# Places in SBUF: two pools trade places, odd-sized tiles are put together, V weight rows become 640 columns wide

## The chip, the cores and the metric

The kernel runs on one core of one Trainium2 chip. The metric is the device time of one execution in microseconds (us), lower is better. The kernel before took 1538.11 us as the median of three runs (1535.11, 1538.11 and 1538.29); the execution that the profiler recorded took 1535.44 us.

## The reference

One decoder layer over 1024 tokens of width 1024, all in float32. Two attentions run side by side and are merged by gates; a SwiGLU feed-forward network follows. Cut to what matters:

```python
h = rms_norm(x, norm_mix_g[layer])
proj = h @ w_in[layer]                      # q, k, v of both attentions, forget logits, gates
...
o_g, lse_g = dilated_window_attention(...)  # three groups (window, dilation), four heads each
y_a = o_a.reshape(b, s, DIL_OUT_WIDTH).astype(x.dtype) @ w_dil_out[layer]
o_b = forgetting_attention(fox[:, :, 0], fox[:, :, 1], fox[:, :, 2], jax.nn.log_sigmoid(f_logit))
y_b = o_b.reshape(b, s, FOX_WIDTH).astype(x.dtype) @ w_fox_out[layer]
x = x + (g_a * y_a + g_b * y_b).astype(x.dtype) @ w_out[layer]
h2 = rms_norm(x, norm_ffn_g[layer])
gu = h2 @ w_ffn_in[layer]                   # 1024 -> 2 x 2816
x = x + (jax.nn.silu(gu[..., :D_FF]) * gu[..., D_FF:]) @ w_ffn_down[layer]
return rms_norm(x, norm_final_g)
```

The forgetting attention adds a running sum of `log_f` over the tokens to its scores; the kernel computes that sum with a triangular matrix of ones (`upper`).

## The kernel before, in words

**Products in three parts.** A float32 operand is split into a rounded high part and the rest, both of type fp32r (`split`, lines 91 to 93: ScalarE writes the high part, VectorE the low one). A product is then three matmuls: high by high, high by low, low by high (`mm3`, `projT`, `prod`). Nearly all of TensorE's work is such matmuls of 128 x 128 weights with a moving operand of 512 columns. Each is a load of its weights (PEld in the profile) and a matmul (PE); the load for the next matmul runs while the matmul before it streams its columns.

**Stages, in order of time.** (1) Tokens are normalised and transposed into `hT_t`, which stays in SBUF as moving operand; V of the forgetting attention is computed beside it (`values`), there with `hT_t` as weights and the V weights `wv` as moving operand of 256 and 264 columns. (2) The running sum of the forget logits. (3) Forgetting attention, four pairs of heads; q and k come from `projT` with weights from `wpool`. (4) Dilated attention. (5) Gates and merge (`merge`, weights from `wpool`). (6) The output projection (`w_out`), here with `hT_t` as weights and `w_out` as moving operand, of `w_out` the first four of eight tiles in the contraction out of `wpool`. (7) The feed-forward products: two plain columns of tiles (`plain`), then twenty in a scheme of seven products (`up`), of which the two with `A1` take their weights from `wpool`. (8) The down projection, added up in nine groups; the first group uses `wpool` for both operands.

**Filler.** `ahead` computes q and k of the dilated attention and the gates in advance: 28 calls, each 2 halves of the weights by 2 halves of the tokens by 4 tiles by 3 matmuls, from its own pool at the right end of SBUF (`fw`), into its own two banks (`pf`). They are scheduled between the work of stages 1 to 5.

**Order.** A scheduler at build time sets each engine's order; at run time an engine takes its instructions in that order and waits on semaphores.

**Places.** Pools are stacked: those on the left side from low addresses up, in the order in which they are entered (lines 72 to 76: `cpool`, `wpool`, `small`, `hpool`), those on the right side from the end down. A tile takes a multiple of 32 bytes of each partition. Below, *residue* is a tile's byte address in a partition modulo 512. `cpool` holds `ident` (512 bytes), `epst` (32), `ones` (512), `bg` (64) and `bf` (32), 1152 together, so what comes behind it has another residue than what stands before it. In the right-hand pools no tile has an odd size, but SBUF's end has residue 480. `load_w` (line 103) allocates a weight tile of `kt` rows of `n` columns; for V of the forgetting attention `n` is 520, so a row is 2080 bytes, and each next row's residue is 32 more.

Of the kernel before, what the change touches and what calls it, by code (L numbers as in the profile page):

```python
# [8 lines left out]
F32 = mybir.dt.float32  # L9
F32R = mybir.dt.float32r  # L10
I32 = mybir.dt.int32
AF = mybir.ActivationFunctionType
ALU = mybir.AluOpType
PSUM = bass.MemoryType.PSUM

P = 128
# [3 lines left out]
NT = S // P  # L20
# [27 lines left out]
def layer_kernel(  # L48
# [16 lines left out]
    nc = tc.nc  # L65
    x, out, w_in, w_dil_out, w_fox_out = x[0], out[0], w_in[0], w_dil_out[0], w_fox_out[0]
    w_out, w_ffn_in, w_ffn_down = w_out[0], w_ffn_in[0], w_ffn_down[0]

    def pool_of(name, bufs, side="left"):
        return tc.tile_pool(name=name, bufs=bufs, side=side, reuse_waits="tile")  # L70

    cpool = ctx.enter_context(tc.tile_pool(name="cpool", bufs=1))
    wpool = ctx.enter_context(tc.tile_pool(name="wpool", bufs=2))
    small = ctx.enter_context(tc.tile_pool(name="small", bufs=4))
    h_ctx = pool_of("hpool", 1)
    hpool = h_ctx.__enter__()
    psd = ctx.enter_context(tc.tile_pool(name="psd", bufs=6, space=PSUM))
# [6 lines left out]
    def nm(s):  # L84
        uid[0] += 1
        return f"{s}_{uid[0]}"

    def pd():
        return psd.tile([P, HALF], F32, tag="d", name=nm("pd"))
# [13 lines left out]
    def load_w(src, kt, n, tag="w", bufs=2, pool=None, chunk=None, rpool=None, rbufs=2, shared=0, between=None):  # L103

        pool = pool or wpool
        hi = pool.tile([P, kt, n], F32R, tag=tag + "h", name=nm("wh"), bufs=bufs)
        lo = pool.tile([P, kt, n], F32R, tag=tag + "l", name=nm("wl"), bufs=bufs)
        chunk = chunk or n
        for c0 in range(0, n, chunk):
            cs = slice(c0, min(n, c0 + chunk))  # L110
            own = rpool and c0 >= shared
            raw = (rpool if own else wpool).tile([P, kt, cs.stop - c0], F32, tag="wr", name=nm("wr"),
                                                 bufs=rbufs if own else 2)
            last_w[0] = nc.sync.dma_start(out=raw[:], in_=src[:, cs].rearrange("(k p) c -> p k c", p=P))
            if between and c0 == chunk:
                between()
            split(hi[:, :, cs], lo[:, :, cs], raw[:])
        return Pair(hi, lo)
# [4 lines left out]

    ident = cpool.tile([P, P], F32, name="ident")
    make_identity(nc, ident[:])
    epst = cpool.tile([P, 1], F32, name="epst")
    nc.gpsimd.memset(epst[:], EPS)
    def load_gain(pool, g):
# [137 lines left out]
    with pool_of("fox", 1) as spool:  # L266
        lf = spool.tile([P, NT, 8], F32, name="lf", bufs=1)

        with pool_of("foxv", 2) as vpool:
            xts, last_x = [], [None]  # L270

            def load_x():
                i = len(xts)
                if i < NT:
                    xts.append(vpool.tile([P, D], F32, tag="xt", name=nm("xt"), bufs=4))
                    last_x[0] = nc.sync.dma_start(out=xts[i][:], in_=x[i * P:(i + 1) * P, :])

            load_x()
            gain1 = load_gain(vpool, norm_mix_g)
            ones = cpool.tile([P, P], F32, name="ones")  # L280
            nc.gpsimd.memset(ones[:], 1.0)
            upper = spool.tile([P, P], F32, name="upper", bufs=1)
            nc.gpsimd.memset(upper[:], 1.0)
            nc.gpsimd.affine_select(out=upper[:], in_=upper[:], compare_op=ALU.is_ge, fill=0.0,
                                    base=0, pattern=[[1, P]], channel_multiplier=-1)
            vf = spool.tile([P, NT, 4, 2, DH], F32, name="vf", bufs=1)
            bg = cpool.tile([P, 16], F32, name="bg")
            bf = cpool.tile([P, 8], F32, name="bf")
            nc.gpsimd.dma_start(out=bf[0:1, :], in_=b_fgt[0:1, :])
            with nc.allow_non_contiguous_dma("per-partition gate bias"):  # L290
                nc.gpsimd.dma_start(out=bg[:], in_=b_gate[0].rearrange("(k p) -> p k", p=P))
            nc.gpsimd.partition_broadcast(bf[:], bf[0:1, :])
            wv = load_w(w_in[:, FOX0 + 2 * FOX_W:GATE0], KT, FOX_W + 8, tag="wv", bufs=1, pool=vpool,
                        chunk=P, rpool=vpool, rbufs=3, shared=2 * P, between=load_x)

            def values(i):
                hh, c = divmod(i * P, HALF)
                for c0, n in ((0, 256), (256, 264)):
                    pv = pd()
                    for k in range(KT):  # L300
                        mm3(pv[:, :n], hT[hh][:, k, c:c + P], wv[:, k, c0:c0 + n], k == 0, k == KT - 1)
                    p0 = c0 // 128
                    nc.vector.tensor_copy(
                        vf[:, i, p0:p0 + 2],
                        pv[:, :256].rearrange("p (a b d) -> p a b d", a=2, b=2))
                    if n == 264:
                        nc.vector.tensor_tensor(out=lf[:, i, :], in0=pv[:, 256:264], in1=bf[:],
                                                op=ALU.add)

            for i in range(NT):  # L310
                load_x()
                hh, c = divmod(i * P, HALF)
                norm_transpose(xts[i][:], gain1, hT[hh], c, vpool, False)
                if i > 0:
                    values(i - 1)
            values(NT - 1)

        az = spool.tile([P, NT * 8], F32, name="az", bufs=1)
        u = spool.tile([P, NT * 8], F32, name="u", bufs=1)
        t1 = spool.tile([P, NT * 8], F32, name="t1", bufs=1)  # L320
        z = lf[:].rearrange("p a b -> p (a b)")
        nc.vector.tensor_scalar(out=t1[:], in0=z, scalar1=-1.0, scalar2=None, op0=ALU.mult)
        nc.vector.tensor_tensor(out=az[:], in0=z, in1=t1[:], op=ALU.min)
        nc.scalar.activation(out=az[:], in_=az[:], func=AF.Exp)
        nc.vector.tensor_scalar(out=u[:], in0=az[:], scalar1=1.0, scalar2=None, op0=ALU.add)
        nc.vector.tensor_scalar(out=t1[:], in0=u[:], scalar1=-1.0, scalar2=None, op0=ALU.add)
        nc.vector.tensor_tensor(out=az[:], in0=az[:], in1=t1[:], op=ALU.subtract)
        nc.vector.reciprocal(out=t1[:], in_=u[:])
        nc.vector.tensor_tensor(out=az[:], in0=az[:], in1=t1[:], op=ALU.mult)
        nc.scalar.activation(out=u[:], in_=u[:], func=AF.Ln)  # L330
        nc.vector.tensor_tensor(out=az[:], in0=az[:], in1=u[:], op=ALU.add)
        nc.vector.scalar_tensor_tensor(out=z, in0=z, scalar=0.0, in1=az[:],
                                       op0=ALU.min, op1=ALU.subtract)

        pc = pd()
        nc.tensor.matmul(pc[:, 0:64], upper[:], z, start=True, stop=True)
        nc.tensor.matmul(pc[:, 64:128], ones[:], z, start=True, stop=True)
        tot = spool.tile([P, NT, 8], F32, name="tot", bufs=1)
        negc = spool.tile([P, NT, 8], F32, name="negc", bufs=1)
        nc.vector.tensor_copy(tot[:], pc[:, 64:128].rearrange("p (a b) -> p a b", a=NT))  # L340
        for i in range(1, NT - 1):
            nc.vector.tensor_tensor(out=tot[:, i, :], in0=tot[:, i, :], in1=tot[:, i - 1, :], op=ALU.add)
        nc.vector.tensor_scalar(out=negc[:, 0, :], in0=pc[:, 0:8], scalar1=-1.0, scalar2=None,
                                op0=ALU.mult)
        nc.vector.scalar_tensor_tensor(out=negc[:, 1:, :],
                                       in0=pc[:, 8:64].rearrange("p (a b) -> p a b", b=8), scalar=-1.0,
                                       in1=tot[:, 0:NT - 1, :], op0=ALU.mult, op1=ALU.subtract)

        def fox_proj(pool, ql, pr):

# [118 lines left out]
    with pool_of("dil", 1) as spool:  # L469
# [4 lines left out]
        with pool_of("dilm", 1) as mpool:  # L474
# [5 lines left out]
                                    pattern=[[1, 256]], channel_multiplier=-1)  # L480
            nc.gpsimd.affine_select(out=R0[:], in_=R0[:], compare_op=ALU.is_ge, fill=BIG, base=P,
                                    pattern=[[-1, 256]], channel_multiplier=1)
            nc.gpsimd.affine_select(out=R2[:], in_=R2[:], compare_op=ALU.is_ge, fill=BIG, base=0,
                                    pattern=[[1, P]], channel_multiplier=-1)
# [6 lines left out]
                                           op0=ALU.mult, op1=ALU.add)  # L491
# [5 lines left out]
                                    pattern=[[-1, 2], [1, 256]], channel_multiplier=-2)  # L497
            nc.gpsimd.affine_select(out=R1[:], in_=R1[:], compare_op=ALU.is_ge, fill=BIG, base=P,
                                    pattern=[[1, 2], [-1, 256]], channel_multiplier=2)
# [4 lines left out]
        with pool_of("dilv", 1) as vpool:  # L504
            for g0, ng in ((0, 1), (1, 2)):
                c0, n = 2 * DIL_W + g0 * 256, ng * 256
# [380 lines left out]
    with pool_of("down", 1) as fpool:  # L887
        acc = fpool.tile([P, NT, D], F32, name="acc", bufs=1)
        for gi, grp in enumerate(groups):
# [9 lines left out]
            for t in range(NT):  # L899
# [22 lines left out]
                if last:  # L922
# [4 lines left out]
                    for ch in range(2):  # L927
# [3 lines left out]
                        else:  # L931
                            nc.vector.tensor_scalar(out=xf[:, cs], in0=xf[:, cs], scalar1=r[:, 0:1],
                                                    scalar2=None, op0=ALU.mult)
# [30 lines left out]
```

## Time and profile before

| what | value |
|---|---|
| median of three runs | 1538.11 us |
| the profiled execution's own time | 1535.44 us |
| its span, first to last instruction | 1533.7 us |
| TensorE matmul busy | 1500.8 us, 98% of the span |
| VectorE, ScalarE, GpSimd busy | 840.7, 525.6, 353.8 us |
| mean granted TensorE clock | 0.994 |

The 1.7 us between the span and the execution's time lie around the first and the last instruction. Busy time of PE is modelled at the end of each matmul: a matmul's duration overlaps the next one's start, so the time that a matmul takes from a stream is the distance of two starts, called *pitch* below, and not its duration.

### The profile page before, as it was taken

The page shows a single profiled execution, that of the slowest core. Times are in us where ns is not written, and L with a number is a line of the kernel's source. Part 1 is how long each engine was busy: PE and PEld are TensorE (multiplying, and loading weights), DVE is VectorE, ACT ScalarE, POOL GpSimd, SP SyncE. Part 2 cuts the span into 40 slices and gives each one's busy share as a digit, 9 for nine tenths or more (in the row PEclk, how much of TensorE's full clock was granted, in tenths as well). Part 3 has the DMA queues.
Part 4 walks back from the last instruction along what each step waited for, and adds up shares of the span by engine and source line. Part 5 has one row for each costly group of instructions (what it writes and reads, how often), then busy time and mean ns, then how long its engine had stood idle before and what let it go on. Part 6 is the DMA issues. An engine that isn't in the chain of part 4 may idle for free.

```text
span 1533.7 us, 18441 instructions
## 1 busy us (share of the span) xinstructions
PE 1500.8 (98%) x7172; PEld 1215.8 (79%) x7172; DVE 840.7 (55%) x1329; ACT 525.6 (34%) x828; POOL 353.8 (23%) x302
## 2 busy tenths in 40 slices
PE   6999999999999999999999999999999999999997
PEld 6987777777996777888888778888888887788886
DVE  6438677683129983114726854344444445956546
ACT  5245556553003234323414332222222224312113
POOL 1012224231001110000000145555555553140000
PEclk9999999999999999999999999999999999999999
DMA  8021211134213125433713122222222225642302
GB/s 258 5 62 56 67 58 42 35 90 129 71 35 131 56 76 198 129 104 130 257 56 137 42 69 83 82 83 82 82 83 83 82 89 193 211 139 83 96 14 96
DMA packets 130471, 148.56 MB, mean 97 GB/s; under 512 B 6352, under 2 KB 104656, under 8 KB 130384
## 3 DMA queue, kind: packets, MB, share of 16 engines
q1 hardware_dynamic: 117712, 103.86, 22.0%
q10 hardware_dynamic: 6768, 22.55, 4.1%
q0 software_dynamic: 5904, 20.98, 3.6%
q8 instruction: 56, 0.92, 0.2%
q14 instruction: 31, 0.25, 0.1%
HBM read 109.62 MB, written 37.75 MB: 96 GB/s over the span
## 4 chain that ended last, share of the span: by engine, by line
PE 94%; DVE 2%; DMA 1%; ACT 1%; issue 1%; SPq 0%; POOL 0%; ACTq 0%; DVEq 0%
PE pd L769 24%; PE pd L96 10%; PE pd L97 10%; PE pd L98 10%; PE pf L96 7%; PE pf L97 7%; PE pf L98 7%; PE pd L184 4%; PE pd L185 4%; PE pd L188 4%; PE pd L443 2%; PE pd L257 1%; PE pd L392 1%; PE pd L393 1%; PE pd L627 1%; PE pt L166 1%
## 5 line engine op out<-in xcount | busy, mean ns | idle before, releaser
L92 ACT ACTIVATE wh<-wr 128x1024 fp32r<-128x1024 f32 (+2 forms) x187 | 155.1, 837 | 475.1 <-PE pf L97 158.0
L93 DVE TENSOR_TENSOR wl<-wr,wh 128x1024 fp32r<-128x1024 f32 (+2 forms) x187 | 180.1, 969 | 206.9 <-ACT wh L92 202.5
L769 PE MATMUL pd<-hT_t,wh 128*128 128x512 f32 x640 | 200.8, 395 | 2.2 <-ACT c L855 2.2
L96 PE MATMUL pf<-hT_t,wh 128*128 128x512 f32 x448 | 180.1, 402 | 0.0
L97 PE MATMUL pf<-hT_t,wh 128*128 128x512 f32 x448 | 179.7, 401 | 0.0
L98 PE MATMUL pf<-hT_t,wl 128*128 128x512 f32 x448 | 177.1, 400 | 0.0
L769 PE MATMUL pd<-tT,wh 128*128 128x512 f32 x480 | 148.4, 390 | 0.4 <-DVE v L773 0.4
L769 PEld LDWEIGHTS pd<-hT_t,wh 128*128 128x128 f32 x640 | 121.1, 189 | 29.1 <-ACT c L855 2.6
L96 PE MATMUL pd<-wh,wh 128*128 128x512 f32 x352 | 137.4, 391 | 3.1 <-DVE acc L915 1.8
L98 PE MATMUL pd<-wh,wl 128*128 128x512 f32 x352 | 137.0, 389 | 0.0
L97 PE MATMUL pd<-wl,wh 128*128 128x512 f32 x352 | 137.0, 389 | 0.0
L96 PE MATMUL pd<-wh,hT_t 128*128 128x512 f32 (+2 forms) x384 | 129.2, 346 | 3.6 <-ACT wh L92 3.1
L97 PE MATMUL pd<-wl,hT_t 128*128 128x512 f32 (+2 forms) x384 | 131.6, 343 | 0.9 <-DVE t L150 0.7
L98 PE MATMUL pd<-wh,hT_t 128*128 128x512 f32 (+2 forms) x384 | 131.2, 342 | 0.0
L769 PE MATMUL pd<-hT_t,wl 128*128 128x512 f32 x320 | 126.1, 395 | 0.0
L915 DVE TENSOR_TENSOR acc<-pd,acc 128x512 f32<-128x512 f32 x128 | 85.6, 685 | 68.3 <-PE pd L98 68.3
L839 POOL TENSOR_TENSOR s<-wr 128x512 f32<-128x512 f32 x20 | 33.2, 1660 | 335.8 <-DVE tT L93 268.7
L769 PEld LDWEIGHTS pd<-tT,wh 128*128 128x128 f32 x480 | 90.0, 188 | 20.1 <-DVE v L773 0.8
L96 PEld LDWEIGHTS pf<-hT_t,wh 128*128 128x128 f32 x448 | 85.2, 190 | 23.0 <-issue 2.5
L98 PEld LDWEIGHTS pf<-hT_t,wl 128*128 128x128 f32 x448 | 85.0, 190 | 23.0 <-issue 3.1
L97 PEld LDWEIGHTS pf<-hT_t,wh 128*128 128x128 f32 x448 | 85.2, 190 | 22.2 <-issue 2.7
L769 PE MATMUL pd<-tT,wl 128*128 128x512 f32 x240 | 93.5, 390 | 0.0
(197 smaller groups left out, 2652.2 us busy)
## 6 DMA issues: line engine op xcount, KB each, us to landing
wr<-in_w_ffn_in_dram SPq DMA_DIRECT2D x44, 512.0 KB, 3.7
wr<-in_w_in_dram SPq DMA_DIRECT2D x56, 256.0 KB, 3.1
wr<-a_dram SPq DMA_DIRECT2D x22, 512.0 KB, 4.2
wr<-in_w_ffn_down_dram SPq DMA_DIRECT2D x22, 512.0 KB, 3.7
a_dram<-a POOLq DMA_DIRECT2D x20, 512.0 KB, 4.8
wr<-in_w_in_dram SPq DMA_DIRECT2D x18, 512.0 KB, 4.4
g_dram<-fst ACTq DMA_DIRECT2D x16, 512.0 KB, 3.2
land<-g_dram SPq DMA_DIRECT2D x16, 512.0 KB, 3.4
```

Source lines behind the costliest of these rows:

```text
L92: nc.scalar.activation(out=hi, in_=src, func=AF.Copy)
L93: nc.vector.tensor_tensor(out=lo, in0=src, in1=hi.bitcast(F32), op=ALU.subtract)
L96: nc.tensor.matmul(psum, w.hi, m.hi, start=start, stop=False)
L97: nc.tensor.matmul(psum, w.hi, m.lo, start=False, stop=False)
L98: last_mm[0] = nc.tensor.matmul(psum, w.lo, m.hi, start=False, stop=stop)
L184: nc.tensor.matmul(pt[hh][:], w.hi[:, k], m.hi, start=(k == 0), stop=False)
L185: nc.tensor.matmul(pt[hh][:], w.hi[:, k], m.lo, start=False, stop=False)
L188: nc.tensor.matmul(pt[hh][:], w.lo[:, k], m.hi, start=False, stop=(k == kt - 1))
L443: nc.tensor.matmul(po[half[e], HALF - width[j]:], vf[:, j, pr, e], L[:, off[j]:off[j + 1]], start=(j == nj - 1), stop=(j == 0), skip_group ...
L769: last_mm[0] = nc.tensor.matmul(bank[:], p, q, start=first and k == 0 and n == 0, stop=k == 3 and n == 2, skip_group_check=True)
L839: nc.gpsimd.tensor_tensor(out=s12[:, :4], in0=u1, in1=u2, op=ALU.add)
L915: nc.vector.tensor_tensor(out=acc[:, t, cs], in0=pt[:], in1=acc[:, t, cs], op=ALU.add)
```

## The change

It moves tiles in SBUF and pads one kind. The pool `wpool` is entered ahead of `cpool`; `ones` is allocated behind `ident`; a tile `right` of 88 columns (352 bytes) stands at the right end of SBUF and is set to zero on GpSimd; `load_w` rounds the columns of a weight row up to a multiple of 128, which changes V of the forgetting attention alone (520 to 640); `upper`, `az`, `u`, `t1` and `tot` move from the pool `fox` into a pool `cums` of their own, which is left before the attention's pool `foxa` is entered, so that the two share their place. `negc` stays in `fox`.

```diff
+    wpool = ctx.enter_context(tc.tile_pool(name="wpool", bufs=2))
     cpool = ctx.enter_context(tc.tile_pool(name="cpool", bufs=1))
-    wpool = ctx.enter_context(tc.tile_pool(name="wpool", bufs=2))
     small = ctx.enter_context(tc.tile_pool(name="small", bufs=4))
+    right = ctx.enter_context(tc.tile_pool(name="right", bufs=1, side="right")).tile([P, 88], F32, name="right")
+    nc.gpsimd.memset(right[:], 0.0)
...
-        hi = pool.tile([P, kt, n], F32R, tag=tag + "h", name=nm("wh"), bufs=bufs)
-        lo = pool.tile([P, kt, n], F32R, tag=tag + "l", name=nm("wl"), bufs=bufs)
+        row = -(-n // P) * P
+        hi = pool.tile([P, kt, row], F32R, tag=tag + "h", name=nm("wh"), bufs=bufs)
+        lo = pool.tile([P, kt, row], F32R, tag=tag + "l", name=nm("wl"), bufs=bufs)
...
     make_identity(nc, ident[:])
+    ones = cpool.tile([P, P], F32, name="ones")
...
-            ones = cpool.tile([P, P], F32, name="ones")
             nc.gpsimd.memset(ones[:], 1.0)
-            upper = spool.tile([P, P], F32, name="upper", bufs=1)
-            nc.gpsimd.memset(upper[:], 1.0)
-            nc.gpsimd.affine_select(out=upper[:], in_=upper[:], compare_op=ALU.is_ge, fill=0.0,
-                                    base=0, pattern=[[1, P]], channel_multiplier=-1)
...
-        az = spool.tile([P, NT * 8], F32, name="az", bufs=1)
...
+        negc = spool.tile([P, NT, 8], F32, name="negc", bufs=1)
+        with pool_of("cums", 1) as cums:
+            upper = cums.tile([P, P], F32, name="upper", bufs=1)
+            nc.gpsimd.memset(upper[:], 1.0)
+            nc.gpsimd.affine_select(out=upper[:], in_=upper[:], compare_op=ALU.is_ge, fill=0.0, base=0,
+                                    pattern=[[1, P]], channel_multiplier=-1)
+
+            az = cums.tile([P, NT * 8], F32, name="az", bufs=1)
...
```

The rest of the diff is the computation of the running sum, word for word, indented under `cums`. Where the tiles stand, by the two built programs (byte address in a partition, and its residue):

| tiles | before | after |
|---|---|---|
| `wpool`: raw weights `wr` | 17664, 21760 (256) | 16512, 20608 (128) |
| `wpool`: `wh`, `wl` | 25856 to 38144 (256) | 24704 to 36992 (128) |
| `ahead`: `wh`, `wl` of `fw` | 208864 to 215008 (480) | 208512 to 214656 (128) |
| V weights `wv`, high and low | 147584 (128), 164224 (384), rows of 2080 | 146048 (128), 166528 (128), rows of 2560 |
| `ones` | 17056 (160) | 41600 (128) |
| `hT_t` | 43136 (128) | 43136 (128) |
| `tT`, the other weights of stages 4, 6, 7 and 8 | (128) | (128) |
| `vf`, V of the forgetting attention | 109440 (384) | 108928 (384) |

On TensorE, VectorE, ScalarE and SP the instructions stand in the same order as before. On GpSimd the head of the program differs. Its rows before, from the first after the constants on (`bf` and `bg` are biases, `ql` the low part of the queries; line numbers are those of the kernel before):

```order
L281 MEMSET ones 128x128
L283 MEMSET upper 128x128
masks.py:199 ISA
masks.py:199 AFFINE_SELECT ident<-ident 128x128
L289 DMA bf<-in_b_fgt_dram 1x8x1
L291 DMA bg<-in_b_gate_dram 128x16x1
L284 AFFINE_SELECT upper<-upper 128x128
L292 ISA
L292 ISA bf<-bf 128x8
L455 MEMSET ql_836 64x1024
L455 MEMSET ql_837 64x1024
```

The same stretch of the changed program, with its own line numbers:

```order
L285 MEMSET ones 128x128
L289 DMA bf<-in_b_fgt_dram 1x8x1
L291 DMA bg<-in_b_gate_dram 128x16x1
masks.py:199 ISA
masks.py:199 AFFINE_SELECT ident<-ident 128x128
L292 ISA
L292 ISA bf<-bf 128x8
L320 MEMSET upper 128x128
L321 AFFINE_SELECT upper<-upper 128x128
L460 MEMSET ql_845 64x1024
L460 MEMSET ql_846 64x1024
```

The two writes of `upper` moved behind the broadcast of `bf`, since they now wait until a buffer of `x` tiles that lay there is free; the two small DMAs moved ahead of `ident`. The first write of `ql` now waits for the end of the running sum (TensorE, VectorE and ScalarE), whose tiles it overwrites, where it waited for the `x` tiles before; the first write of `ql` on VectorE (line 360) waits for GpSimd.

## Rows read from the trace of the kernel before

**Rows 1.** The page: busy time by engine, and the granted clock in 40 slices.
```profile
PE 1500.8 (98%) x7172; PEld 1215.8 (79%) x7172; DVE 840.7 (55%) x1329; ACT 525.6 (34%) x828; POOL 353.8 (23%) x302
PEclk9999999999999999999999999999999999999999
```
**Rows 2.** The page: the chain that ended last, its share of the span by engine.
```profile
PE 94%; DVE 2%; DMA 1%; ACT 1%; issue 1%; SPq 0%; POOL 0%; ACTq 0%; DVEq 0%
```
**Rows 3.** Waits of PE: the longest and the shortest of twelve (total, times, longest).
```profile
PE pt L166 <- DVE hn L161: 9.9, 1, 9.9
...
PE pd L96 <- DVE gt L773: 0.2, 1, 0.2
```
**Rows 4.** Stretches of PE without a wait: length, busy (instructions), clock, DMA share, GB/s.
```profile
563.06:581.57 18.51, 18.51 (x80) 1.00 0.36 100
697.79:747.28 49.49, 49.49 (x214) 1.00 0.52 175
747.51:763.31 15.80, 15.80 (x69) 1.00 0.95 350
1308.99:1524.81 215.82, 215.82 (x953) 1.00 0.32 105
908.51:922.15 13.64, 13.64 (x61) 1.00 0.24 70
```
**Rows 5.** Timeline of PE, first down group: start, duration, line, operands.
```profile
1275.96 0.39 PE L97 MATMUL pd<-wl,wh 128*128 128x512 f32 x1
...
1277.78 0.40 PE L98 MATMUL pd<-wh,wl 128*128 128x512 f32 x1
```
**Rows 6.** Groups of PE: names, shape, count, busy, mean ns, idle before.
```profile
L96 PE MATMUL pf<-hT_t,wh 128*128 128x512 f32 x448 | 180.1, 402 | 0.0
L769 PE MATMUL pd<-hT_t,wh 128*128 128x512 f32 x640 | 200.8, 395 | 2.2 <-ACT c L855 2.2
L769 PE MATMUL pd<-tT,wh 128*128 128x512 f32 x480 | 148.4, 390 | 0.4 <-DVE v L773 0.4
L184 PE MATMUL pd<-hT_t,wh 128*128 128x512 f32 x160 | 63.6, 398 | 0.0
L184 PE MATMUL pd<-oh,wh 128*128 128x512 f32 x96 | 37.4, 394 | 0.0
L446 PE MATMUL pd<-Mx,ones 128*64 128x512 f32 x32 | 8.3, 598 | 0.0
L630 PE MATMUL pd<-Mx,ones 128*64 128x512 f32 x16 | 4.2, 600 | 0.0
```
**Rows 7.** Stretches of PE with narrow moving operands, columns as in rows 4.
```profile
63.28:66.13 2.85, 2.85 (x26) 1.00 0.00 0
66.13:69.05 2.92, 2.92 (x27) 1.00 0.00 0
377.36:398.96 21.60, 21.60 (x181) 1.00 0.32 97
```
**Rows 8.** Timeline around the running sum: start, duration, instruction.
```profile
33.31 0.95 POOL L455 MEMSET ql<- 64x1024 f32 x1 [20.74 <-DMA wr<-in_w_in_dram]
77.71 0.33 PE L336 MATMUL pd<-lf,upper 128*128 128x64 f32 x2
79.77 0.22 DVE L345 SCALAR_TENSOR_TENSOR negc<-pd,tot 128x56 f32<-128x56 f32 x1
91.28 1.27 DVE L360 SCALAR_TENSOR_TENSOR ql<-pd,qx 64x512 fp32r<-64x512 f32 x2
```
**Rows 9.** DMA issues: count, KB each, median us from issue to landing.
```profile
wr<-in_w_in_dram SPq DMA_DIRECT2D x56, 256.0 KB, 3.1
wr<-in_w_fox_out_dram SPq DMA_DIRECT2D x8, 256.0 KB, 3.5
```
**Rows 10.** One stretch, dilated attention: PE, PEld, DVE, ACT, POOL busy; clock; DMA.
```profile
500.00:550.00 50.00, 50.00 (x297) 36.05 (x296) 46.17 (x78) 15.68 (x25) 7.32 (x4) 1.00 0.24 74
```

**Rows 11.** The same view, of the filler's tile `pf` alone: busy (matmuls), clock, DMA.
```profile
450.00:600.00 150.00, 103.15 (x409) 0.99 0.29 94
```

More of the change, by code (lines that the diff above doesn't have):

```diff
@@ L316, in layer_kernel @@
             values(NT - 1)
-        az = spool.tile([P, NT * 8], F32, name="az", bufs=1)
[L319 to L338, printed above, removed]
-        negc = spool.tile([P, NT, 8], F32, name="negc", bufs=1)
-        nc.vector.tensor_copy(tot[:], pc[:, 64:128].rearrange("p (a b) -> p a b", a=NT))
-        for i in range(1, NT - 1):
-            nc.vector.tensor_tensor(out=tot[:, i, :], in0=tot[:, i, :], in1=tot[:, i - 1, :], op=ALU.add)
@@ L343, in layer_kernel @@
[L343 to L347, printed above, removed]
+        negc = spool.tile([P, NT, 8], F32, name="negc", bufs=1)
+        with pool_of("cums", 1) as cums:
[4 more added lines that the diff above has]
+            az = cums.tile([P, NT * 8], F32, name="az", bufs=1)
+            u = cums.tile([P, NT * 8], F32, name="u", bufs=1)
+            t1 = cums.tile([P, NT * 8], F32, name="t1", bufs=1)
+            z = lf[:].rearrange("p a b -> p (a b)")
+            nc.vector.tensor_scalar(out=t1[:], in0=z, scalar1=-1.0, scalar2=None, op0=ALU.mult)
+            nc.vector.tensor_tensor(out=az[:], in0=z, in1=t1[:], op=ALU.min)
+            nc.scalar.activation(out=az[:], in_=az[:], func=AF.Exp)
+            nc.vector.tensor_scalar(out=u[:], in0=az[:], scalar1=1.0, scalar2=None, op0=ALU.add)
+            nc.vector.tensor_scalar(out=t1[:], in0=u[:], scalar1=-1.0, scalar2=None, op0=ALU.add)
+            nc.vector.tensor_tensor(out=az[:], in0=az[:], in1=t1[:], op=ALU.subtract)
+            nc.vector.reciprocal(out=t1[:], in_=u[:])
+            nc.vector.tensor_tensor(out=az[:], in0=az[:], in1=t1[:], op=ALU.mult)
+            nc.scalar.activation(out=u[:], in_=u[:], func=AF.Ln)
+            nc.vector.tensor_tensor(out=az[:], in0=az[:], in1=u[:], op=ALU.add)
+            nc.vector.scalar_tensor_tensor(out=z, in0=z, scalar=0.0, in1=az[:],
+                                           op0=ALU.min, op1=ALU.subtract)
+            pc = pd()
+            nc.tensor.matmul(pc[:, 0:64], upper[:], z, start=True, stop=True)
+            nc.tensor.matmul(pc[:, 64:128], ones[:], z, start=True, stop=True)
+            tot = cums.tile([P, NT, 8], F32, name="tot", bufs=1)
+            nc.vector.tensor_copy(tot[:], pc[:, 64:128].rearrange("p (a b) -> p a b", a=NT))
+            for i in range(1, NT - 1):
+                nc.vector.tensor_tensor(out=tot[:, i, :], in0=tot[:, i, :], in1=tot[:, i - 1, :], op=ALU.add)
+            nc.vector.tensor_scalar(out=negc[:, 0, :], in0=pc[:, 0:8], scalar1=-1.0, scalar2=None,
+                                    op0=ALU.mult)
+            nc.vector.scalar_tensor_tensor(out=negc[:, 1:, :],
+                                           in0=pc[:, 8:64].rearrange("p (a b) -> p a b", b=8), scalar=-1.0,
+                                           in1=tot[:, 0:NT - 1, :], op0=ALU.mult, op1=ALU.subtract)
```

## The prediction

> **What bounds the kernel now.** I read the page's busy times first: PE is busy for 1500.8 us of 1533.7 and its clock is granted in full in all 40 slices [rows 1]. Then the chain that ended last: 94% of it is PE, no other engine has more than 2% [rows 2]. Then PE's waits: twelve, from 9.9 us down to 0.2, 24.6 us together [rows 3]. So TensorE's stream sets the end, and what shortens or lengthens a matmul in it counts once. The change takes away no matmul and moves none, so I looked for what sets the pitch (distance of two starts) of matmuls of one shape, 512 columns of fp32r, in stretches where PE never waits [rows 4]. One instruction of each count began before its window, so n is one less than shown.
>
> - 563.06 to 581.57, filler: 18.51 us / 79 = 234.3 ns.
> - 697.79 to 747.28, merge: 49.49 / 213 = 232.3 ns.
> - 747.51 to 763.31, output projection with weights from `wpool`: 15.80 / 68 = 232.4 ns.
> - 1308.99 to 1524.81, down projection: 215.82 / 952 = 226.7 ns.
> - 908.51 to 922.15, feed-forward: 13.64 / 60 = 227.3 ns.
>
> With the table of places this sorts itself. While a matmul streams, the weights of the next are loaded, so I take the difference of the next weights' residue and the streaming operand's. It is 480 − 128 = 352 in the filler, 256 − 128 = 128 in the merge, 128 − 256 = 384 (modulo 512) in the output projection, and 0 in the two fast stretches. It isn't the residue 128 itself: in the first down group both operands lie at 256, and from 1275.96 to 1277.78 eight pitches take 1.82 us, 227.5 ns [rows 5]. It isn't other traffic either: the third stretch runs at 350 GB/s and 0.95 DMA share, the second at 175 GB/s, with one pitch; the fastest stretch has 105 GB/s, the slowest 100.
>
> The Trainium skill speaks against this change here: "TensorE: Matmul & The Clock Gate", in "Step-by-step: what each phase is for", says that the engine reads weights and moving operand through two independent ports, and that loading the next tile's weights takes no read bandwidth from the running matmul. By that the places could not matter and the change would bring nothing. The trace differs: 234.3 and 232.3 against 226.7 ns for one shape; still, that the place is the cause is an inference from stages that differ in more than their places, so the rule stays as a rival below.
>
> **The change part by part.** By the table every fp32r pair of matmul and next weights gets difference 0, but for the dilated V whose weights are every eighth token; those don't change.
>
> 1. Filler: 28 calls x 48 = 1344 matmuls, three lines of 448 [rows 6]. From 234.3 down to 226.7 to 227.3: 7.0 to 7.6 ns each, 9.4 to 10.2 us.
> 2. Weights from `wpool` under `hT_t` or the attention's output: 3 x (160 + 96) = 768 in `projT` [rows 6], 96 in the first plain column of tiles, and 480 in `prod` (`A1`: 20 x 24; they stand in the `hT_t` groups of line 769, whose mean duration is 395 ns against 390 of the `tT` group, which has none [rows 6]). 1344 x 5.0 to 5.6 ns = 6.7 to 7.5 us.
> 3. Output projection: 2 x 2 x 4 x 4 x 3 = 192 matmuls with difference 384; 5.1 to 5.7 ns, 1.0 to 1.1 us.
>
> I take the lower ends, since 227.3 is the pitch in a stage with as much work beside it as these have: 9.4 + 6.7 + 1.0 = 17.1 us.
>
> 4. V weights: 384 matmuls of 256 and 264 columns, now at scattered differences. From 63.28 to 66.13, 24 of 256 columns, 2.85 us, 118.8 ns; from 66.13 to 69.05, 24 of 264 columns, 2.92 us, 121.7 ns (the counts show two that began before, and the one that begins at the end). The dilated group 0 has 256 columns at difference 0: 21.60 / 180 = 120.0 ns [rows 7]. So alike is no gain for narrow operands: 192 x 1.2 = 0.2 us lost, and for 264 columns between 120.0 (none) and 120.0 x 264/256 = 123.8 ns: from 0.3 us gained to 0.4 lost. I take +0.4 together; bounds −0.1 and +0.6.
> 5. `ones`: 48 float32 matmuls, 12.5 us of busy time together [rows 6]. Difference 32 before, 0 after. No row shows a float32 matmul at both; if they gained as the filler does, 48 x 7.6 = 0.4 us; I take 0.
> 6. GpSimd's head: one write more and two DMAs ahead of `ident`, while PE waits for VectorE until 9.9 us [rows 3]; 0. `upper` waits for the buffer that `ql` waited for before, free at 33.31, and PE reads it at 77.71: 44 us of cover. `ql` now waits until the running sum ends, 79.77 + 0.22 = 80.0, two writes of 0.95 end near 82; VectorE's line 360, which now waits for the first, started at 91.28 since its product is not done before [rows 8]. Cover 9 us; without it VectorE's queue (the splits of the next weights) and then PE would stand for what is missing, about 2 us at most.
> 7. The loads into `wpool` land at residue 128, no longer at 256. 256 KB into the filler's pool (residue 480) take 3.1 us, 256 KB of `w_fox_out` into `wpool` (256) 3.5 [rows 9]: the load off a 256-byte boundary is no slower; 0. The Trainium skill, "DMA: Bandwidth & Descriptors", "How a descriptor splits into AXI transactions", has it otherwise: a descriptor that doesn't start on a multiple of 256 bytes pays beats for bytes it doesn't use, 20 for 16 here by my estimate; the trace does not show that. If these loads cost a quarter more, the few that PE waits for would lose about 2 us.
> 8. What doesn't arrive: around 500 us VectorE is busy 46.17 of 50 us [rows 10], so part of the filler's gain there can turn into waits for VectorE. 450 to 600 us holds 409 filler matmuls [rows 11], at 7.0 ns 2.9 us; I lose 0.6 of it.
>
> Sum: −17.1 + 0.4 + 0.6 = −16.1 us. From the profiled execution's 1535.44 that gives 1519.3. The three runs have a mean of 1537.2, 1.7 above it: 1521.
>
> **The rivals.**
>
> *The fillers' gain is lost.* They fill PE's time beside the attentions; if VectorE's and ScalarE's chain there paces the stage, a faster filler makes a longer wait. For: VectorE at 46 of 50 us. Against: PE has no long wait in those stages now, and their VectorE work starts from PE's results. Only terms 2 and 3 and the two losses stay: −7.7 + 1.0 = −6.7, 1528.7, with the 1.7 1530. If half is lost, 1526.
>
> *The place is not the cause.* Pitch belongs to the stage (which banks, which pattern of three), as the two-port rule would have it. For: each difference but 0 occurs mainly in one stage. Against: rows 5, and that the three differences give 234.3, 232.3 and 232.4 while the two fast stretches are different code. Then 0 to +0.4: 1535.4 to 1535.8, 1537 with the 1.7.
>
> *Alike is worse.* The one comparison in which an aligned pair is slower is the narrow one, 120.0 against 118.8 ns [rows 7]. If that were the rule, with weights and moving operand meeting in one place, and the fast stretches fast for another reason, the 2880 wide and 384 narrow ones would pay 1.2 ns: +3.9 us, 1539.3, 1541 with the 1.7. It decides from the point at which the filler's pitch comes out above 234.3. Against it stand the fast stretches, all at difference 0.
>
> *It doesn't do what it says.* By the two programs' addresses it does, in all 2880 pairs; that rival is out.
>
> **How the numbers follow.** Forecast 0.72 (1516 to 1524). A part or all of the fillers' gain lost 0.14 (1524 to 1531). Not the place 0.08. Alike is worse 0.04. More than forecast, by 226.7 everywhere and a gain at the 264 columns, 0.02 (18.8 us, 1516 and below). Below 0.2%, 3.1 us, this kernel's measurement can't tell a change: its three runs spread over 3.2 us. Faster 0.72 + 0.14 + 0.02 = 0.88, same 0.08, slower 0.04. The range reaches from 1514, the largest sum under the lowest run (1535.1 − 18.8 = 1516.3, and 2 for that spread), to 1531, the lost filler; it leaves out the last two cases, about 0.12 with the tails.
>
> **What would show it.** Right: in the changed profile stretches of filler, merge and output projection without waits have a pitch of 226.7 to 227.5 ns; the mean durations of the `pf` groups fall from 402 to about 390; V at 256 columns stands at 120.0; `hT_t` groups of line 769 at 390. Step 8: waits of PE for VectorE between 450 and 560 us of 1 us or less in sum above today's. Step 6: line 360 does not wait for GpSimd. Wrong would be: a filler pitch still above 231 (not the place), or 227 with new waits of PE for VectorE or ScalarE of many us (gain lost), or wide matmuls above 232 (alike is worse).

## The result and the profile after

The changed kernel takes 1522.59 us (median of 6 runs, 1521.37 to 1524.68), the kernel before on the same chip 1538.18 (6 runs, 1535.11 to 1539.68): ratio 0.9904, 95% interval 0.9891 to 0.9917. Forecast were 1521.0 and a range of 1514 to 1531. The profiled execution took 1523.66 us. The times of one kernel spread with TensorE's granted clock: of 47 further runs of the kernel before, the nine with a mean of 0.992 took 1538.8 to 1539.8 us, the sixteen with 0.996 or more 1533.4 to 1537.6.

Busy time and clock, on the page of the changed kernel, against [rows 1]:

```profile
PE 1486.5 (98%) x7172; PEld 1213.7 (80%) x7172; DVE 841.7 (55%) x1329; ACT 526.0 (35%) x828; POOL 355.9 (23%) x303
PEclk9999999999999999999999999999999999999999
```

PE has the same 7172 matmuls and 14.3 us less to do. The clock looks the same, but a 9 in this row stands for 90% or more of a slice of some 38 us, so it hides short stretches at half clock; they come up below. The stretches of PE without a wait, in the order of [rows 4] (filler, merge, output projection, down, feed-forward) and then of [rows 7] (V with 256 columns, V with 264, dilated group 0): length, busy (instructions), clock, DMA share, GB/s.

```profile
556.15:574.08 17.93, 17.93 (x80) 1.00 0.36 103
687.27:736.23 48.96, 48.96 (x217) 1.00 0.55 181
736.86:752.96 16.10, 16.10 (x72) 1.00 0.92 344
1297.23:1513.04 215.81, 215.81 (x953) 1.00 0.31 103
894.72:908.31 13.59, 13.59 (x61) 1.00 0.28 77
64.29:67.15 2.86, 2.86 (x26) 1.00 0.00 0
67.15:70.03 2.88, 2.88 (x26) 1.00 0.00 0
371.90:393.48 21.58, 21.58 (x181) 1.00 0.38 111
```

With one instruction less than shown (two less for V): filler 17.93 / 79 = 227.0 ns (234.3 before), merge 48.96 / 216 = 226.7 (232.3), output projection 16.10 / 71 = 226.8 (232.4), down 215.81 / 952 = 226.7 (226.7). All wide fp32r work with contiguous weights now has one pitch. V with 256 columns went from 118.8 to 119.2 ns, with 264 columns from 121.7 to 120.0. Groups of PE, against [rows 6]: mean ns of one behind the comma.

```profile
L774 PE MATMUL pd<-hT_t,wh 128*128 128x512 f32 x640 | 198.4, 391 | 2.4 <-ACT c L860 2.4
L99 PE MATMUL pf<-hT_t,wh 128*128 128x512 f32 x448 | 177.0, 395 | 0.0
L189 PE MATMUL pd<-hT_t,wh 128*128 128x512 f32 x160 | 62.8, 393 | 0.0
```

The chain that ended last has changed too; in [rows 2] PE had 94% and DMA 1%:

```profile
PE 89%; DMA 3%; ACT 2%; DVE 2%; POOL 2%; issue 1%; SPq 1%; ACTq 0%; DVEq 0%
```

Both programs issue the same matmuls in one order, so the two traces can be laid side by side, start by start. Where two starts lie under 260 ns apart in both, the change of their distance is pitch. The rest holds the waits, and also matmuls that ran at half clock.

| pairs, by difference before | pairs | ns before | ns after | us |
|---|---|---|---|---|
| filler, 352 | 1252 | 234.1 | 227.5 | −8.2 |
| weights from `wpool`, 128 | 1285 | 232.5 | 227.2 | −6.8 |
| output projection, 384 | 192 | 232.8 | 226.9 | −1.1 |
| alike before too, 0 | 2524 | 227.5 | 226.9 | −1.7 |
| narrow (V) | 653 | | | −0.3 |
| V with strided weights | 190 | 244.4 | 244.4 | 0.0 |
| longer distances: waits, half clock | 286 | | | +6.4 |

So 18.1 us came from the pitch, and 6.4 were lost again. The loss lies in three places: about 1 us in the first 50 us, 4.2 us in the feed-forward stage (900 to 1250 us), 2 us in the first groups of the down projection.

Not all of it is waiting. In the first down groups PE waits for `acc` 1.8 us in before and 2.3 in after, and 0.7 us behind that wait its granted clock falls from 2.4 to 1.2 GHz (half of full) for 3.4 us in after, which makes 1.4 of the 2 us, while in before it stays up. The same 3.4 us, first of after, then at the same matmuls of before:

```profile
1293.20:1296.60 3.40, 3.40 (x10) 0.51 0.58 218
```

```profile
1306.50:1309.90 3.40, 3.40 (x15) 1.00 0.56 201
```

Another 0.6 of the 4.2 us is a half-clock stretch that both kernels have, but which hits later matmuls after the change, some of them behind the line at 900 us. The other 3.5 us are waits. They show in what PE's weight loads wait for there (total, times, longest; the matmuls running meanwhile cover a part of it), first of before, then of after:

```profile
PEld pd L769 <- DVE wl L93: 0.7, 4, 0.2
```

```profile
PEld pd L774 <- DVE wl L96: 5.8, 14, 0.6
```

What PE's weight load waits for is shown by one round of the feed-forward loop in after's timeline (start, duration, engine, line, output and input; in brackets the idle time before it and its releaser):

```profile
1046.37 0.62 ACT L876 ACTIVATE sg<-gt 128x512 f32<-128x512 f32 x1
1047.06 2.27 POOL L877 TENSOR_TENSOR sg<-gt,sg 128x512 f32<-128x512 f32 x1 [1.77 <-ACT sg L876]
1049.31 1.28 POOL L848 TENSOR_TENSOR s<-wr,wr 128x512 f32<-128x512 f32 x1
...
1050.61 1.62 SPq L759 DMA_DIRECT2D wr<-in_w_ffn_in_dram  x2
...
1054.56 1.06 ACT L95 ACTIVATE wh<-wr 128x1024 fp32r<-128x1024 f32 x1 [2.89 <-DMA wr<-in_w_ffn_in_dram]
1055.65 1.23 DVE L96 TENSOR_TENSOR wl<-wr,wh 128x1024 fp32r<-128x1024 f32 x1 [3.26 <-ACT wh L95]
...
1056.92 0.19 PEld L774 LDWEIGHTS pd<-hT_t,wl 128*128 128x128 f32 x1 [0.48 <-DVE wl L96]
```

It is a loop through five engines: a product and a difference on GpSimd release the raw tile, the load is issued at 1050.61, its data split by ScalarE and VectorE, and TensorE comes 0.48 us too early for `wl`. The stage saved 3.3 us of pitch and gave them back here: with the 4.2 us it got 0.9 us longer, 0.3 without the stretch of half clock.

### The profile page after: what moved, and what is told of

Read it like the earlier page. It is cut to its first block, busy times and chain, and to the rows that moved or that the text cites. A ratio compares the mean times of both kernels' runs of the same rounds, so it can differ in the third digit from the quotient of the medians.

```text
span 1522.0 us, 18443 instructions
## 1 busy us (share of the span) xinstructions
PE 1486.5 (98%) x7172; PEld 1213.7 (80%) x7172; DVE 841.7 (55%) x1329; ACT 526.0 (35%) x828; POOL 355.9 (23%) x303
## 4 chain that ended last, share of the span: by engine, by line
PE 89%; DMA 3%; ACT 2%; DVE 2%; POOL 2%; issue 1%; SPq 1%; ACTq 0%; DVEq 0%
PE pd L774 20%; PE pd L99 10%; PE pd L100 10%; PE pd L101 10%; PE pf L99 7%; PE pf L100 7%; PE pf L101 7%; PE pd L189 4%; PE pd L193 4%; PE pd L190 4%; PE pd L448 2%; DMA wr<-in_w_ffn_in_dram 2%; ACT wh L95 1%; PE pd L262 1%; PE pd L397 1%; PE pd L398 1%
## 5 line engine op out<-in xcount | busy, mean ns | idle before, releaser
L99 PE MATMUL pf<-hT_t,wh 128*128 128x512 f32 x448 | 177.0, 395 | 0.0
L100 PE MATMUL pf<-hT_t,wh 128*128 128x512 f32 x448 | 176.7, 394 | 0.0
```

The costliest lines, as they stand in the source:

```text
L99: nc.tensor.matmul(psum, w.hi, m.hi, start=start, stop=False)
L100: nc.tensor.matmul(psum, w.hi, m.lo, start=False, stop=False)
```

## The experiments

Two theories for the new waits stood against each other. **A**: the raw loads, now at residue 128, start off a 256-byte boundary and land later. **B**: the feed-forward loop was already as slow as TensorE, and any quicker pitch waits for it. All kernels have one order of matmuls.

**The changed kernel again.**

> The changed kernel once more, beside the other three on one chip. Every theory: 1522 to 1524 us, 0.990 of the kernel before, with the pitches of its first profile (226.8 ns in filler, merge and output projection) and about 4 us of new waits in the feed-forward stage from 900 to 1250 us.

Measured: 1524.57 us (1523.12 to 1526.55), ratio 0.9915 (0.9901 to 0.9929); waits for `wl` in the feed-forward stage 5.4 us in 14 times. The new waits repeat. In the first groups of the down projection it lost 2.6 us against the first profile of before: 1.4 by another 3.4 us at half clock, the rest by a wait for `acc` of 3.0 us instead of 1.8.

**All at 256.**

```diff
+    left = ctx.enter_context(tc.tile_pool(name="left", bufs=1)).tile([P, 32], F32, name="left")
+    nc.gpsimd.memset(left[:], 0.0)
     wpool = ctx.enter_context(tc.tile_pool(name="wpool", bufs=2))
...
-    right = ... .tile([P, 88], F32, name="right")
+    right = ... .tile([P, 56], F32, name="right")
```

> The changed kernel with every tile moved by 128 bytes: weights, operands and raw weights all lie at 256 modulo 512 instead of all at 128, so the pairs stay alike and the raw loads begin on a 256-byte boundary again. Theory A (the new waits of 4 us in the feed-forward stage, 1 us at the start and 2 us in the first down groups come from raw loads that land later off that boundary): the w_ffn_in loads land in 3.7 us as before and not in 4.2, the long gaps of 900 to 1250 us fall from 4.2 to under 1.5 us, the time to 1516 to 1519. Theory B (the loop that prepares the weights is at its limit because TensorE got faster, wherever the loads land): the waits stay and the time is 1521.5 to 1524. If the residue itself (256 and not 128) mattered to the matmuls, the pitch of the filler would leave 226.8 ns.

Measured: 1520.93 us (1520.46 to 1522.6), ratio 0.9889 (0.9875 to 0.9902), between the two theories. Looking at each place by itself separates them. At the start A holds. One row, the matmul of the running sum, stands at the end of the V work, so its start tells how long the start took; in before it is at 77.71 [rows 8]. In after, then in this kernel:

```profile
78.47 0.33 PE L342 MATMUL pd<-lf,upper 128*128 128x64 f32 x2
```

```profile
76.94 0.33 PE L344 MATMUL pd<-lf,upper 128*128 128x64 f32 x2
```

1.5 us earlier with the loads on the boundary (those of `x` and of V's raw weights too, which before and after have at residue 128). In the feed-forward stage most of what A says fails; the waits are nearly those of after:

```profile
PEld pd L776 <- DVE wl L98: 4.8, 14, 0.6
```

Start by start the stage is 0.6 to 0.9 us shorter than in the two profiles of the changed kernel; two profiles of one kernel differ by as much, so this is not shown to be the boundary. The filler's stretch has 227.0 ns, so 128 or 256 is the same to the matmuls.

**Only the raw tiles at 128.** The kernel before with the raw weights in a pool of their own ahead of the others; `wh` and `wl` keep their places.

```diff
+    rawpool = ctx.enter_context(tc.tile_pool(name="rawpool", bufs=2))
     cpool = ctx.enter_context(tc.tile_pool(name="cpool", bufs=1))
...
-            raw = (rpool if own else wpool).tile(...
+            raw = (rpool if own else rawpool).tile(...
```

> The kernel before with nothing changed but the place of the raw weights (w_in, w_ffn_in and the first down groups), 256 to 128 modulo 512, off the 256-byte boundary; every matmul has its residues of before. Theory A: the loads land 0.3 to 0.5 us later, with new waits at the start (1 us) and in the first down groups (2 us), and in the feed-forward stage, where TensorE is slower than after and so the loop has more room, 0 to 4 us; 1539 to 1545 us. Theory B: 1538 us as the kernel before, within 1 us, and no new waits.

Measured: 1539.82 us (1537.79 to 1543.02, 11 runs), ratio 1.0018 (1.0008 to 1.0028): slower by 1.2 to 4.3 us with the wide pitches of before to 0.1 ns. The two loads into the moved tiles that are issued between 14 and 17 us, while others are still under way (count, KB, median us from issue to landing), in before, here and in the kernel with all at 256:

```profile
wr<-in_w_in_dram SPq DMA_DIRECT2D x2, 512.0 KB, 7.3
```

```profile
wr<-in_w_in_dram SPq DMA_DIRECT2D x2, 512.0 KB, 8.0
```

```profile
wr<-in_w_in_dram SPq DMA_DIRECT2D x2, 512.0 KB, 7.1
```

Over all twelve profiles these two take 6.8 to 7.3 us with `wpool`'s raw tiles on a 256-byte boundary (seven profiles) and 7.9 to 8.0 off it (five). The running sum's matmul starts at 78.97 here, 1.26 us after that of before. So the residue of a load's target counts where loads queue behind one another and PE waits for them.

The feed-forward stage has a share in it that the runs don't settle: this execution's weight loads wait for `wl` 4.1 us there in 14 times, before's 0.7 and, in the second profile below, 3.1. Start by start the stage is 1.7 us longer than in the first of these and 0.8 us longer than in the second.

**Only the filler.** The kernel before with nothing but the tile on the right.

```diff
+    right = ctx.enter_context(tc.tile_pool(name="right", bufs=1, side="right")).tile([P, 88], F32, name="right")
+    nc.gpsimd.memset(right[:], 0.0)
```

> The kernel before with only the tile on the right, which moves the filler's weights from 480 to 128 modulo 512. If the difference of residues is what costs, the filler's 1344 pairs give up 352 for 0: pitch 234.3 to 226.9 ns there, while merge and output projection stay at 232.4; 8.2 us from the matmul-by-matmul comparison of before and after (9.4 by the prediction), so 1528.5 to 1531. Theories A and B agree here: raw loads stay at 256, the feed-forward stage keeps its pitch for the A1 pairs and gets no new waits. If the places were not the cause, 1538.

Measured: 1531.18 us (1528.58 to 1532.52), ratio 0.9952 (0.994 to 0.9965), 0.2 above the expected range. Filler, then merge, in the columns of [rows 4]:

```profile
557.01:574.93 17.92, 17.92 (x80) 1.00 0.37 103
688.55:738.05 49.50, 49.50 (x214) 1.00 0.53 175
```

17.92 / 79 = 226.8 ns in the filler, 49.50 / 213 = 232.4 in the merge: the code of both is that of before. The tile moved what stands at the right end of SBUF, of the matmuls' operands the filler's weights alone, and one pitch changed with it. That ends the rival that the pitch belongs to the stage. Start by start, the 1252 filler pairs give 7.9 us.

**All but the filler.** The kernel with all at 256, without the tile on the right.

> All the rest of the change without the filler: the kernel with every tile at 256 modulo 512, but without the tile on the right, so that the filler's weights lie at 480 under an operand at 256, a difference of 224 in 1252 compared pairs (352 before). The pairs with weights from the padded, moved pool go from 128 and 384 to 0. If only the difference of residues counts, merge and output projection fall from 232.4 to 226.8 ns, 8.0 us together, pairs that were alike give 1.6 us, and the filler keeps 232 to 234 ns. Theory A (raw loads on their 256-byte boundary, no new waits): 1527.5 to 1529. Theory B (the feed-forward stage is at its limit as soon as its matmuls are quick, 3.3 us of waits as in the kernel with all at 256): 1530 to 1533.

Measured: 1526.74 us (1524.98 to 1528.98), ratio 0.9933 (0.9919 to 0.9947). Filler and merge again:

```profile
557.77:576.19 18.42, 18.42 (x80) 1.00 0.36 101
691.80:740.07 48.27, 48.27 (x214) 1.00 0.55 177
```

233.2 and 226.6 ns, the other way round. Waits for `wl` in the feed-forward stage: 4.0 us in 13 times, though the loads lie on the boundary; that is B. The time is below both ranges. A part of that is the clock. Against the first profile of before this execution is 1.5 us quicker near 470 us and 1.5 us near 896, since before is at half clock there,

```profile
469.80:473.20 3.40, 3.40 (x10) 0.50 0.97 305
896.40:899.80 3.40, 3.40 (x10) 0.50 0.70 208
```

and this execution, like some others here, is not. How much of the median that explains is not shown; the mean clocks of its six runs go from 0.993 to 0.997.

**A sweep of the difference.** The changed kernel, without the tile on the right, and with the filler's weight rows padded:

```diff
-        hi = pool.tile([P, kt, row], F32R, tag=tag + "h", name=nm("wh"), bufs=bufs)
-        lo = pool.tile([P, kt, row], F32R, tag=tag + "l", name=nm("wl"), bufs=bufs)
+        if tag == "fw":
+            turn[0] ^= 1
+            pads = ((4, 8), (8, 0))[turn[0] ^ 1]
+            hi, lo = [pool.tile([P, kt, row + pad], F32R, tag=f"fw{c}{turn[0]}", name=nm("w" + c), bufs=1)
+                      for c, pad in zip("hl", pads)]
```

> The changed kernel without the tile on the right, and with rows of the filler's weights padded by 0, 16 or 32 bytes, so that one run has thirteen differences of residue in the filler's pairs: 32, 48, 64, 80, 96, 128, 160, 192, 224, 256, 288, 320 and 352, some 50 to 220 pairs of each. If any difference costs: all at 232 to 235 ns but none at 227. If it is a slope: pitch grows from 227 with the difference. If the period is 256 and not 512: 256 at 227 and 320 like 64. If 64-byte lines are what counts: 64 and its multiples differ from 32, 48 and 80. Time between 1522 and 1533, by the mean pitch.

Measured: 1530.04 us (1529.06 to 1535.1). The profiled execution took 1535.1, with more time at half clock than any other here; distances over 262 ns are left out below, and with them the matmuls at half clock. Mean pitch by difference, from the starts of its matmuls and the addresses in the program (51 to 213 pairs each, 3971 at 0):

```
difference  0      32     48     64     80     96     128    160    192    224    256    288    320    352
ns          227.1  232.6  231.3  231.5  231.3  230.7  232.6  234.6  228.1  233.2  230.3  232.3  230.7  231.4
```

A step, not a slope: 32 bytes cost 5.5 ns and 352 cost 4.3. 256 costs 3.2, so the period is not 256. Nor is it longer than 512: in the quickest kernel below, 2626 pairs that are alike modulo 1024 have 227.0 ns, and 2643 that differ by 512 have 227.0. One value stands out, 192 with 228.1 in 53 pairs; all but one of them follow one difference (80), so this run can't say which of the two is the reason. The multiples of 64 do not stand apart from 32, 48 and 80, and most values lie below the 232 to 235 that I expected.

**The product on VectorE, from before.** B says that the loop's length is the limit, so the next kernels shorten it and leave the places alone.

```diff
-            nc.gpsimd.tensor_tensor(out=sg2[:], in0=gt2[:], in1=sg2[:], op=ALU.mult)
+            nc.vector.tensor_tensor(out=sg2[:], in0=gt2[:], in1=sg2[:], op=ALU.mult)
```

> The kernel before with one product per feed-forward block (gt2 times sigmoid, 20 in all) moved from GpSimd to VectorE, so that the raw weights are free about 2 us earlier. Theory B says the loop has just enough room at the slow pitch, so nothing is gained: 1537 to 1539, ratio 0.999 to 1.001, weight loads of TensorE waiting for wl at most 0.7 us as before. Were the loads the limit already, it would gain.

Measured: 1535.9 us (1533.09 to 1538.09, 12 runs), ratio 0.999 (0.9981 to 0.9999): 0.2 to 2.9 us gained, and below the expected range. The loop of before was at its limit a little, not with room to spare. In this kernel no weight load of the feed-forward stage waits for `wl`.

**The same product, from the kernel with all at 256.**

> The kernel with every tile at 256 and the same product moved to VectorE. Theory B (the loop GpSimd product, GpSimd difference, load, ScalarE, VectorE, TensorE is the limit of the quick feed-forward stage): the next loads start about 2 us earlier, TensorE's waits for wl in that stage fall from 4.8 us to under 1, the long gaps of 900 to 1250 from 3.3 to under 1 us, time 2.5 to 3.5 us below the kernel with all at 256, so 1517 to 1519. If the landing of the loads and not their start were the limit, or VectorE became late with its own work, no gain: 1521.

Measured: 1516.94 us (1516.28 to 1518.25), ratio 0.9867 (0.985 to 0.9884); 4.0 us under the kernel with all at 256, and the quickest of all. 900 to 1250 us of PE, first of the kernel with all at 256, then of this one:

```profile
900.00:1250.00 350.00, 349.21 (x1529) 1.00 0.26 82
```

```profile
900.00:1250.00 350.00, 350.00 (x1546) 1.00 0.26 83
```

17 matmuls more in the same time, 3.9 us at 226.8 ns; no weight load waits for `wl` there any more. One round of its loop:

```profile
1043.80 0.62 ACT L878 ACTIVATE sg<-gt 128x512 f32<-128x512 f32 x1
...
1045.54 0.68 DVE L879 TENSOR_TENSOR sg<-gt,sg 128x512 f32<-128x512 f32 x1
1045.70 1.67 POOL L850 TENSOR_TENSOR s<-wr,wr 128x512 f32<-128x512 f32 x1 [2.98 <-DVE wl L98]
...
1047.40 1.61 SPq L761 DMA_DIRECT2D wr<-in_w_ffn_in_dram  x2
...
1052.14 1.23 DVE L98 TENSOR_TENSOR wl<-wr,wh 128x1024 fp32r<-128x1024 f32 x1 [2.32 <-ACT wh L97]
```

From the start of the sigmoid to the load it is 3.60 us, in after 4.24 (1046.37 to 1050.61); to the end of `wl` 9.57 against 10.51. I had expected 2 us: GpSimd's difference now waits for VectorE's `wl` instead of the product. 0.9 us was enough, since TensorE had missed by half a microsecond. The loads land no sooner than in after: the median in this stage is 4.4 us here and 4.2 there.

**The kernel before, a second profile.**

> The kernel before, unchanged, with a second profile. All eight kernels so far spend 2.4 to 4.2 us more than the first profile of before in the first groups of the down projection, the ones whose matmuls and loads there are those of before too. If that profile was a lucky execution, this one shows the same 2 to 3 us there and a span of 1536 to 1538 us; if before is really quicker there, the stretch is as in the first profile.

Measured: 1536.83 us, span 1535.1. It loses 1.1 us in the first down groups against the first profile of before, and its weight loads wait longer in the feed-forward stage:

```profile
PEld pd L769 <- DVE wl L93: 3.1, 12, 0.4
```

The 1.1 us are the wait for `acc`, 2.9 us here for 1.8; the clock stays up behind it. So no part of after's loss in the first down groups is shown to come from the places: 1.4 us are half clock, and its wait of 2.3 us lies between those of two executions of before. Some of the waits for `wl` are chance too: the loop of before waits 0.7 us in one execution and 3.1 in another. Against the second, the changed kernel's 5.8 and 5.4 are 2.7 and 2.3 us more.

**The same product, from the changed kernel.**

> The changed kernel (all at 128, raw loads off the 256-byte boundary) with the product on VectorE. Theory B: the waits for wl of the feed-forward stage go, 5.8 to under 1 us, although the loads stay off the boundary; the first 50 us keep their 1.0 us over before. 3 to 4 us below the changed kernel: 1518.5 to 1520.5. Theory A in its first form (loads off the boundary land too late): the loads begin 2 us earlier here too, so half of the waits may stay, 1521 or more.

Measured: 1519.0 us (1516.5 to 1522.41), ratio 0.9885 (0.987 to 0.99). With every raw load still off the boundary the waits for `wl` in the feed-forward stage are gone:

```profile
900.00:1250.00 350.00, 350.00 (x1545) 1.00 0.26 83
```

So in that stage the length of the loop decides, and not the boundary. The same edit is worth 1.6 us by the medians in the kernel before, 4.0 in the kernel with all at 256, and here 3.6 against the first six runs of the changed kernel and 5.6 against the second five: with the quicker matmuls the loop costs more. The start keeps its loss: the running sum's matmul begins at 78.84, against 77.17 in the kernel with all at 256 and the same product.

## Why the prediction was right, and where it was not

The time came out 1.6 us above the forecast, with the mechanism that it named. By its steps (between the two profiled executions):

1. Filler, −9.4 forecast: 8.2 us in 1252 pairs, 6.6 ns each; 8.8 for 1344. The two kernels with one half of the change each show the cause. In the stretch without waits the pitch is as forecast, 227.0; over all pairs it is 227.5, which makes 6.6 ns each and not 7.0. The mean duration of the `pf` groups was put at 390 and is 395.
2. Weights from `wpool`, −6.7: 6.8 in 1285 pairs. `hT_t` of line 769: 391 for a forecast of 390.
3. Output projection, −1.0: −1.1.
4. V, +0.4 taken with a lower bound of −0.1: −0.3 for all narrow pairs. By the stretches 256 columns lost 0.4 ns a pair and 264 gained 1.7, over all pairs 0.7. But the second profile of before, with nothing changed, has −0.7 us in the same pairs against the first, and the second of the changed kernel +0.9, so no effect on narrow operands is shown.
5. `ones`: the two groups have 598 and 600 ns as in [rows 6]; 0.
6. GpSimd's head: line 360 (now 365) starts at 91.83 and waits for no GpSimd.
7. Loads off the boundary, 0 taken: **this step failed**. It compared landings of two different transfers, 3.1 and 3.5 us, in stretches where nothing waits for them, and so saw no price. Where loads queue, at the start, they land in 7.9 instead of 7.3 us, and the running sum of the changed kernel starts 0.8 us later than in before and 1.5 later than with all on the boundary; with only the raw tiles moved it is 1.3 after before. The Trainium skill, "DMA: Bandwidth & Descriptors", "How a descriptor splits into AXI transactions", which the prediction set aside with its 2 us, is right in its direction; it tells of the bytes that a descriptor fetches, and here the target in SBUF moved, so that this is the mechanism is not shown. By the medians the boundary is worth 2.1 us with only the raw tiles moved, and 1.7 or 3.6 between all at 128 (its first and second set of runs) and all at 256. The start holds 0.8 to 1.5 of it; where the rest lies, the traces don't settle.
8. Waits for VectorE around 500 us, 0.6 taken: PE's waits from 450 to 560 us are one of 1.6 us before and after. **The wait was in the wrong stage.** The prediction looked for a full engine (VectorE, 46 of 50 us) and should have looked for a loop: in the feed-forward stage VectorE, ScalarE and GpSimd all have room, but load, split and release form a round that takes as long as TensorE's. The sign stood in the trace of before, four waits for `wl` of 0.7 us in all. 3.5 us went there against the first profile of before, 2.6 against its second.

What it did not see at all: 1.7 us from pairs that were alike before. 1.1 of it lies in the feed-forward stage, where blocks of such pairs alternate with blocks of unlike ones; in the kernel with all at 256 the first two pairs behind an unlike one fell there from 232.9 and 233.6 to 227.7 and 227.2 ns, the 963 from the fifth on by 0.5. And it read the granted clock as full in all 40 slices, where before has 3.4 or 6.8 us at half clock near 364, 470 and 896 us.

That the time fits so well is in part luck. From profile to profile the forecast was −16.1 us and −11.8 came: the pitch gave 1.4 us more than put down (18.1 for 17.1 less 0.4 lost in V), and waits and half clock took 5.8 more (6.4 for 0.6). The medians fell by 15.6, since the first profile of before lay 2.7 us below its median and that of after 1.1 above its own. The allowance of 1.7 us for the first of these went the right way, but it does not make up for the 5.8. Of the rivals, only a part of "the gain is lost" came true, by another chain and in another stage than it said. The rule behind "the place is not the cause", from the Trainium skill, "TensorE: Matmul & The Clock Gate", "Step-by-step: what each phase is for", that loading the next weights takes nothing from the running matmul, does not hold here: 234.1 and 227.5 ns for the same matmuls.

Still open: why unlike residues cost, and the quick 192 of the sweep. In the first down groups every other profile loses 1 to 4 us against the first of before. It does not follow the places: the kernel before with the product on VectorE has all of them and loses 1.7. The wait for `acc` there takes 1.8 to 3.7 us, and the ten other profiles, but neither of before, have 3.4 or 6.8 us at half clock next to it, which cost 0.8 to 2.2 us. Why that wait is longer, and why the clock falls at one such wait and not at another, is open.

## What to carry to other kernels

When PE is the bound and its matmuls of one shape have several pitches, list each stage's pitch beside the residues modulo 512 of the streaming operand and of the next weights; a pool of odd size is a cheap thing to pad, and one kernel with a single residue moved proves it. Before counting the gain, look for the loop that feeds PE with waits of a few tenths already: a stage gains only until that loop is the limit, so shorten it in the same step (here one product on another engine, 4 us). Choose the common residue so that loads too start on a 256-byte boundary: by the medians 256 was worth 1.7 to 3.6 us more than 128. And before a difference of 1 to 3 us between two profiles is put down to the change, look for stretches at half clock in both.

## What the hardware showed

- A wide fp32r matmul's pitch is 226.7 to 227 ns in stretches without waits (up to 227.8 over all pairs of a kind) if the next weights lie like the streaming operand modulo 512 bytes, and 230 to 235 otherwise, with 32 bytes as with 352 (one of thirteen values at 228). Narrow ones, 256 columns, show nothing of it: 118.8 before, 119.2 after.
- Weights read with a stride (every eighth token) have 244.4 ns in all kernels compared, 17 more than contiguous ones of like place.
- 512 KB loads of 512-byte pieces landed in 6.8 to 7.3 us with their target on 256 bytes and in 7.9 to 8.0 off it, where other loads were under way (14 to 17 us). In the feed-forward stage, at a quarter of the DMA engines' time, no such difference shows: 3.7 to 4.4 us on it, 4.0 to 4.5 off it.
- In each profile the granted clock falls to half for 3.4 or 6.8 us in two to five places besides the end. Each of these begins in, or at most 2 us behind, a wait of PE of 1.0 to 4.2 us, but not every such wait has one: in the second profile of before a wait of 2.9 us near 1307 us left the clock at 1.00. A wide matmul's pitch at half clock is 427 ns.
